# Ada-vector dot products with two load tiles of their own, and weight-keeping jobs with single buffers, in a two-layer trunk kernel

## The chip, the cores and the metric

The kernel runs on one core of a Trainium2 chip. The metric is the device time of one execution in microseconds (us). Three timed runs of the kernel before gave 2517.2, 2519.7 and 2522.97 us; their median, 2519.7 us, is the time before.

## The reference

The reference is a decoder trunk for one sequence of 1024 tokens with 1024 channels, in float32. Layer A is a diagonal state-space (S5) mixer with a gated linear unit (GLU) behind it; layer B is stick-breaking attention with 16 heads, whose keys and values come from the residual stream after layer A. Each layer ends with a squared-ReLU MLP of width 4096. Every sub-layer is normed and then shifted and scaled by vectors that come from one conditioning vector `c`:

```python
sh_a, sc_a, g_a, sh_m, sc_m, g_m = ada_chunks(c, ada_w[i], ada_b[i], 6)   # silu(c) @ ada_w[i] + ada_b[i]
h = modulate(rms_norm(x, mix_norm_g[i]), sh_a, sc_a)
mix = val * sigmoid(gate)            # layer A: val, gate = split(gelu(s5(h)) @ s5_w_glu)
x = x + g_a * mix
h = modulate(rms_norm(x, mlp_norm_g[i]), sh_m, sc_m)
x = x + g_m * (square(relu(h @ mlp_w1[i])) @ mlp_w2[i])
```

The products of `silu(c)` with the columns of the ada weights, 14 vectors of 1024 values in all, are matrix-vector products. So are the bias vectors that shift the keys, values and queries.

## The kernel before

The residual stream lies transposed in on-chip memory, as 8 channel tiles by 2 token halves (`xs[k][h]`, 128x512). All large products run on TensorE with every operand split into a rounded part and a rest (`uh` and `ul` for weights, hi and lo for activations), three matmuls for one (`mm3`). A weight unit is 128x1024: `load_unit` loads it on SyncE's queue (SP) into a `raw` tile (512 KB), ScalarE casts it to `uh` (L217), and VectorE subtracts to `ul` (L84). The raw tiles are a ring of three (`raw_tile`), the split ones a ring of three each (`un_tile`).

The stages follow each other: the S5 layer (its instructions in an order written out by hand, `S5_ORDER`, to about 212 us), the GLU (`glu`, 8 channel tiles by 2 halves, to about 417 us), the first MLP (`mlp(0, ...)`, to about 1145 us), the attention (to about 1793 us), its output projection and the second MLP. The first MLP begins with eight half units of up-products (one weight unit each, for one half), and then has 8 blocks `c`; each block is four up units and four down units, in the order in which they are written. Outside the S5 layer nothing but the attention's TensorE stream is pinned to the order written: a planner lays out the order of instructions on each engine by a simulated timeline when the program is built. On the chip each engine then runs its instructions in that fixed order.

Two kinds of side jobs are strewn between the units of the GLU and the first MLP:

- A dot product (`gemv`, L174) loads 128 columns of the transposed ada weights (or of the key, value and query weights) as a 128x1024 raw tile on SP and multiplies it by the broadcast row `silr` with a sum on VectorE (L177). There are 120: 96 on `adaT` and 24 on `wT`. An add of the bias (`fin`) closes each group of eight; `scale_cols` makes scales of some.
- A keeping job (`keep`, L224) prepares half a unit of the attention's weights on GpSimd (POOL): a load from POOL's queue into an `e` tile (L231), a scaling (L78, for keys, values and queries), a cast (L236), a subtraction (L84), and two stores to DRAM (`kh`, `kl`, L239), from which `fetch` takes them in the attention. There are 64. They use four `e` tiles, two for the first half of a unit and two for the second.

`queue` interleaves two jobs of the first kind with one of the second into the list `side`; `pump(n)` emits the next n of them. The GLU pumps nine after each channel tile from the second on, the MLP's `mid` three or four in turn after each down unit and after three of a block's up units. Everything left is emitted in `place(0)` in block 7, behind which the pools `b` and `e` are closed and the pool `late` is opened in their place.

A pool opened with `reuse_waits="tile"` (the helper `tile_pool`, L95) lets a tile wait only for the earlier tiles that lay in the same memory; the default lets it wait for the whole earlier pool that lay there.

Of the kernel before, what the change touches and what calls it, by code (L numbers as in the profile page):

```python
# [8 lines left out]
F32 = mybir.dt.float32  # L9
# [47 lines left out]
def kernel(ctx, tc, A, out):  # L57
# [4 lines left out]
    class Engine:  # L62
        def __init__(self, eng):
            self.eng = eng
# [15 lines left out]
    def add(o, a, b, eng=V):  # L80
        eng.tensor_tensor(o, a, b, op=ALU.add)  # L81
# [13 lines left out]
    def tile_pool(name, bufs=1, **k):  # L95
        return tc.tile_pool(name=name, bufs=bufs, reuse_waits="tile", **k)
# [7 lines left out]

    def open_x(i):
        es = ExitStack()
        pools["x"] = es.enter_context(tile_pool(f"xp{i}", bufs=16 if i else 1))
        pools["raw"] = es.enter_context(tile_pool(f"raw{i}", bufs=3))
        es.callback(pools.pop, "raw")
        turns.clear()  # L110
        return es

    def open_ax(i):
        es = ExitStack()
        pools["ax"] = es.enter_context(tile_pool(f"pax{i}", bufs=4 if "pv" in pools else 6, space=PSUM))
        return es

    cnt = [0]
# [1 line left out]
    def nm(s):  # L120
        cnt[0] += 1
        return f"{s}_{cnt[0]}"
# [9 lines left out]

    def open_pv():
        es = ExitStack()
        pools["pv"] = es.enter_context(tile_pool("ppv", bufs=2, space=PSUM))
        es.callback(pools.pop, "pv")
        return es

# [9 lines left out]
    def raw_tile():  # L148
        return pools["raw"].tile([P, 1024], F32, tag="raw", name=nm("raw"))
# [21 lines left out]
    silc = cp.tile([P, 8], F32, name="silc")  # L171
    kqs = single[:, 1:2]

    def gemv(src, row, bcol):  # L174
        raw = raw_tile()
        SP.dma_start(raw, src)
        V.tensor_tensor_reduce(raw, raw, row, 1.0, 0.0, op0=ALU.mult, op1=ALU.add, accum_out=bcol)  # L177

    def ada_chunk(c0, after=None):
        def one(i):  # L180
            gemv(A["adaT"][i - 16], silr, mod[:, i:i + 1])
# [6 lines left out]
        return [(lambda i=i: one(i)) for i in range(c0, c0 + 8)] + [fin]  # L188

    side = []  # L190

    def pump(n):
        for _ in range(min(n, len(side))):
            side.pop(0)()

    def queue(jobs, n, others):
        while jobs or others:
            side.extend(jobs[:n] + others[:1])
            del jobs[:n], others[:1]
# [24 lines left out]
    def keep(key, src, c, scale=None):  # L224
        if c == 0:
            kept[key] = [dp.tile([P, 1024], F32, name=nm(name)) for name in ("kh", "kl")]
        cs = slice(HN * c, HN * c + HN)
        while len(keeps) < 4:
            keeps.append(fs0.extra((F32, F32R)[len(keeps) % 2]))
        raw, hi = keeps[0:2] if c == 0 else keeps[2:4]  # L230
        G.dma_start(raw, src[:, cs])  # L231
        if scale is not None:
            nk = scale.shape[1] // 2
            r3 = raw.rearrange("p (k m) -> p k m", k=nk)
            mul(r3, r3, scale[:, nk * c:nk * c + nk].unsqueeze(2).broadcast_to([P, nk, HN // nk]), G)
# [25 lines left out]

    def s5(hook):
        es = ExitStack()
        sp = es.enter_context(tile_pool("sp", bufs=1))
        pp = es.enter_context(tile_pool("s5ps", bufs=2, space=PSUM))

        cst = sp.tile([P, C_N], F32, name="cst")
        SP.dma_start(cst, A["cst"])
# [609 lines left out]
    class Inner:  # L878
# [4 lines left out]

        def open(self, name):
            self.es[name] = ExitStack()
            self.pools[name] = self.es[name].enter_context(tile_pool("fp" + name))

        def close(self, *names):
            for name in names:
# [26 lines left out]
    def mlp(layer, xs, hs, norm, fs, mid=None, done=None, place=None):  # L916
# [135 lines left out]
        for h in range(2):  # L1052
            for f in range(4):
                u = load_unit(w1[f])
                plain(0, f, h, up(f, u, h))
                if h == 0 and f == 0:
                    norm.rstd(1)
                elif h == 0 and f == 1:
                    norm.spread(1)
                    norm.apply(1, 0, 8)  # L1060
# [422 lines left out]
        return oh, ou[-2:]  # L1483


    pools["un"] = ctx.enter_context(tile_pool("unp", bufs=3))
# [4 lines left out]
    rowp = ada_es.enter_context(tile_pool("rowp", bufs=1))  # L1491
    silr = rowp.tile([P, D], F32, name="silr")

    def gate(i):
        c = M_GA0 + i
        gemv(A["adaT"][c - 16], silr, mod[:, c:c + 1])
        add(mod[:, c:c + 1], mod[:, c:c + 1], adab[:, c:c + 1])

    first = []

# [19 lines left out]
    ordered[0] = False  # L1520
    hs = [[None, None] for _ in range(8)]
    fs = fs0 = Inner()
    fs.open("a")
    fs.open("e")
    norm = Norm(norm_tiles(fs), xs, hs, 2, M_SHM0)
    with tile_pool("gp", bufs=1) as gp:
        queue(ada_chunk(M_SHM0) + ada_chunk(M_SCM0, lambda: scale_cols(2, M_SCM0)) + ada_chunk(M_GM0), 2,
              [(lambda i=i, c=c: keep(("o", i), A["wo"][i], c)) for i in range(8) for c in range(2)])

        def glu(i, ug, uv, h):  # L1530
            ps = ps_pv if h == 1 and i <= 5 else ps_mm
            pg, pv = ps(), ps()
            for k in range(8):
                mm3(pg, ug, k, ys[k][h], k == 0, k == 7)
            if (i, h) == (6, 1):
                norm.spread(0)
                norm.apply(0, 0, 8)
            for k in range(8):
                mm3(pv, uv, k, ys[k][h], k == 0, k == 7)
            g = gp.tile([P, HN], F32, tag="g", name=nm("g"), bufs=3)  # L1540
# [34 lines left out]
        ts1(kqs, kqs, 0.125, ALU.mult)  # L1575

    def bias_jobs(lo, hi):
        return [(lambda i=i: gemv(A["wT"][i], silr, bias[:, i:i + 1])) for i in range(lo, hi)]

    pump(99)  # L1580
    side.extend(ada_chunk(M_KSC, lambda: scale_cols(4, M_KSC)) + ada_chunk(M_SCA1, lambda: scale_cols(1, M_SCA1)))
    queue(ada_chunk(M_KSH) + ada_chunk(M_SHA1) + ada_chunk(M_GA1) + ada_chunk(M_SHM1)
          + ada_chunk(M_SCM1, lambda: scale_cols(3, M_SCM1)) + ada_chunk(M_GM1)
          + [lambda: shift_row(M_KSH)] + bias_jobs(0, 16)
          + [lambda: shift_row(M_SHA1)] + bias_jobs(16, 24) + [kq_gain], 2,
          [(lambda hp=hp, n=n, c=c: keep(("kv", hp, n), A["wkv"][hp, n], c, scl[:, 32 + 4 * n:36 + 4 * n]))
           for hp in range(8) for n in range(2) for c in range(2)]
          + [(lambda hp=hp, c=c: keep(("q", hp), A["wq"][hp], c, scl[:, 8:16])) for hp in range(8) for c in range(2)])

    brow = cp.tile([P, 2, 128], F32, name="brow")  # L1590

# [18 lines left out]

    def place(k):
        if k == 0:
            pump(999)
            fs.close("b", "e")
            late.append(late_es.enter_context(tile_pool("late", side="right")))
        return late_tile("sg")

# [169 lines left out]
```

## Time and profile before

| | |
|---|---|
| time, median of 3 runs | 2519.7 us (2517.2 to 2522.97) |
| profiled execution, its own time | 2516.43 us |
| span of the profiled execution | 2514.7 us |
| TensorE busy | 2350.6 us, 93% |
| VectorE busy | 1754.3 us, 70% |
| GpSimd busy | 909.5 us, 36% |
| mean granted TensorE clock | 0.974 of full speed |

The span goes from the first to the last instruction. A row of a group names the kernel line, the engine, the operation, the tiles (out<-in), the shape and the count, then the busy time, the mean ns of one, and the idle time of the engine just before them with what ended it. In a timeline row the first two numbers are the start and the length in us, and what stands in brackets is the idle time before it and its releaser. PEclk is the granted clock as a share of 2.4 GHz.

### The profile page before, as it was taken

Reading aid. Unit: us, or ns where it says so; the run is one execution under the profiler, and the core shown is the slowest. Engines: PE = TensorE matmul, PEld = TensorE weight load, DVE = VectorE, ACT = ScalarE, POOL = GpSimd, SP = SyncE. Lnnn points to the kernel's source line nnn. Section 1 sums busy time; section 2 is a strip of 40 time slices with the busy share of each in tenths; the row PEclk is TensorE's granted clock in tenths of the full one; section 3 lists DMA queues with packets and bytes.
Section 4 is the critical chain, followed back from the end, with each engine's and each line's share of the span. In section 5 each row is a group of like instructions: output and inputs, shape, how many; then the busy total and the mean of one; then the engine's idle time right before and its main releaser. Section 6 shows DMA issues by size and latency. Waiting matters only on the chain.

```text
span 2514.7 us, 33271 instructions
## 1 busy us (share of the span) xinstructions
PE 2350.6 (93%) x12552; PEld 1979.3 (79%) x12552; DVE 1754.3 (70%) x2570; ACT 941.8 (37%) x1710; POOL 909.5 (36%) x965
## 2 busy tenths in 40 slices
PE   3888999989999999999899999998999999999998
PEld 2677788867778888888888888887778888888886
DVE  7997557766776545345687877788583667876787
ACT  5653124211111222133566666676351232223221
POOL 4664460378775000014333323343110322342334
PEclk8899999999999999998999999999999999999999
DMA  4225863667766333123211111126721011111112
GB/s 150 86 79 188 283 221 105 216 241 251 252 239 217 101 117 126 45 89 102 81 58 39 64 68 68 59 100 213 250 78 57 34 51 59 60 42 51 56 54 76
DMA packets 105344, 297.08 MB, mean 118 GB/s; under 512 B 13280, under 2 KB 25568, under 8 KB 105184
## 3 DMA queue, kind: packets, MB, share of 16 engines
q1 hardware_dynamic: 87264, 240.42, 27.9%
q0 software_dynamic: 15360, 50.34, 5.5%
q10 hardware_dynamic: 2560, 4.20, 0.7%
q8 instruction: 99, 1.62, 0.3%
q14 instruction: 61, 0.50, 0.1%
HBM read 241.23 MB, written 49.48 MB: 116 GB/s over the span
## 4 chain that ended last, share of the span: by engine, by line
PE 61%; DVE 17%; DMA 11%; issue 5%; ACT 2%; POOL 1%; SPq 0%; DVEq 0%; POOLq 0%; ACTq 0%
DMA raw<-in_adaT_dram 8%; PE pm L70 8%; PE pm L251 8%; PE pm L252 8%; PE pm L253 8%; PE pa L1001 3%; PE pa L999 3%; PE pa L1000 3%; PE pt L70 3%; DVE sn L1282 3%; DVE raw L177 2%; PE pa L253 2%; PE pa L251 2%; PE pa L252 2%; PE po L70 2%
## 5 line engine op out<-in xcount | busy, mean ns | idle before, releaser
L251 PE MATMUL pm<-h,uh 128*128 128x512 f32 x1192 | 465.6, 393 | 19.3 <-ACT rb L927 15.8
L253 PE MATMUL pm<-h,ul 128*128 128x512 f32 x1192 | 465.5, 391 | 4.7 <-DVE ul L84 4.7
L252 PE MATMUL pm<-h,uh 128*128 128x512 f32 x1192 | 466.3, 391 | 1.6 <-DVE h L93 1.6
L217 ACT CAST uh<-raw 128x1024 fp32r<-128x1024 f32 x130 | 136.7, 1051 | 486.9 <-PE pa L252 154.5
L84 DVE TENSOR_TENSOR ul<-raw,uh 128x1024 fp32r<-128x1024 f32 (+1 forms) x158 | 202.7, 1283 | 126.5 <-ACT uh L217 103.8
L251 PEld LDWEIGHTS pm<-h,uh 128*128 128x128 f32 x1192 | 225.0, 189 | 71.5 <-ACT rb L927 19.3
L177 DVE CUSTOM_DVE_ANT_0 raw<-raw,silr 128x1024 f32<-128x1024 f32 x119 | 162.5, 1369 | 155.4 <-DMA raw<-in_adaT_dram 140.6
L253 PEld LDWEIGHTS pm<-h,ul 128*128 128x128 f32 x1192 | 225.1, 189 | 52.5 <-DVE ul L84 5.6
L252 PEld LDWEIGHTS pm<-h,uh 128*128 128x128 f32 x1192 | 225.3, 189 | 48.6 <-DVE h L93 2.2
L70 PE MATMUL pm<-uh,h 128*128 128x256 f32 x1024 | 238.5, 301 | 3.8 <-DVE rs L1138 3.0
L1282 DVE TENSOR_TENSOR_SCAN sn<-sn 128x768 f32<-128x768 f32 (+7 forms) x128 | 180.6, 1417 | 46.5 <-ACT sn L1277 45.2
L81 POOL TENSOR_TENSOR f<-f,f 128x512 f32<-128x512 f32 x30 | 44.0, 1468 | 397.3 <-ACT f L831 397.2
L70 PEld LDWEIGHTS pm<-uh,h 128*128 128x128 f32 x1024 | 181.7, 199 | 5.0 <-DVE rs L1138 3.4
L81 POOL TENSOR_TENSOR raw<-raw 128x256 f32<-128x256 f32 x28 | 26.0, 929 | 411.4 <-DVE ul L84 411.4
L251 PE MATMUL pa<-f,uh 128*128 128x512 f32 x396 | 154.4, 390 | 1.7 <-DVE xall L93 1.0
L252 PE MATMUL pa<-f,uh 128*128 128x512 f32 x396 | 154.1, 389 | 0.0
L253 PE MATMUL pa<-f,ul 128*128 128x512 f32 x396 | 153.7, 389 | 0.0
L70 PE MATMUL pm<-ul,h 128*128 128x256 f32 x512 | 148.7, 290 | 0.9 <-DMA ul<-kl 0.9
L78 POOL TENSOR_TENSOR sg<-sg,sn 128x512 f32<-128x512 f32 x64 | 93.0, 1453 | 122.5 <-DVE sn L1282 56.3
L70 PE MATMUL pm<-h,uh 128*128 128x512 f32 x402 | 133.7, 414 | 0.0
L93 DVE SCALAR_TENSOR_TENSOR x<-pa,mod,x 128x512 f32<-128x512 f32 x143 | 103.3, 743 | 43.5 <-PE pa L253 29.6
L1277 ACT ACTIVATE sn<-z,rrr 128x512 f32<-128x512 f32 (+1 forms) x192 | 111.6, 581 | 46.9 <-PE z L70 45.4
(380 smaller groups left out, 5497.7 us busy)
## 6 DMA issues: line engine op xcount, KB each, us to landing
raw<-in_w_dram SPq DMA_DIRECT2D x140, 512.0 KB, 3.3
raw<-in_adaT_dram SPq DMA_DIRECT2D x96, 512.0 KB, 3.7
uh<-kh SPq DMA_DIRECT2D x40, 512.0 KB, 4.2
ul<-kl SPq DMA_DIRECT2D x40, 512.0 KB, 4.0
kh<-e POOLq DMA_DIRECT2D x64, 256.0 KB, 2.7
kl<-e POOLq DMA_DIRECT2D x64, 256.0 KB, 3.6
raw<-in_wT_dram SPq DMA_DIRECT2D x24, 512.0 KB, 4.3
raw<-in_wglu_dram SPq DMA_DIRECT2D x20, 512.0 KB, 4.7
```

The lines of the kernel that those rows point to most:

```text
L70: return lambda *a, **k: tc.keep_in_program_order(f(*a, **k))
L78: eng.tensor_tensor(o, a, b, op=ALU.mult)
L84: eng.tensor_tensor(o, a, b, op=ALU.subtract)
L93: V.scalar_tensor_tensor(o, a, s, b, op0=op0, op1=op1)
L177: V.tensor_tensor_reduce(raw, raw, row, 1.0, 0.0, op0=ALU.mult, op1=ALU.add, accum_out=bcol)
L217: ACT.copy(uh, raw)
L251: T.matmul(ps, uh[:, sl], hi, start=first, stop=False)
L252: T.matmul(ps, uh[:, sl], lo, start=False, stop=False)
L253: T.matmul(ps, ul[:, sl], hi, start=False, stop=last)
L999: T.matmul(p, uh[:, sl], hi, start=(i == 0), stop=False)
L1277: ACT.activation(g[:, HN * hb + c0:HN * hb + HN], p[:, c0:], AF.Sigmoid, scale=pj.rr[:, 2, t, a:a + 1])
L1282: V.tensor_tensor_scan(g[:, s0:], g[:, s0:], g[:, s0:], 1.0, op0=ALU.mult, op1=ALU.bypass)
```

## The change

Dot products become objects of a class `Gemv` with a `load` of their own. They load into a tile `gv` with two buffers in a new pool `g`, no longer into the raw ring, which in the first part has two tiles in place of three. Two lists, `gems` and `keep_jobs`, take the place of `side`. `pump(ng, nk)` emits ng dot products (and the adds between them), emits the loads of the next two, and emits nk keeping jobs. In the GLU it is called after each half: three dot products in the first channel tile and two in the others, with one keeping job up to the third channel tile and two from the fourth on. In the MLP each of the eight first half units is followed by two dot products, and each `mid` emits two dot products and one keeping job. The gates 1 to 7 of the GLU and the key/value scale (`M_KSC`) move into the list of the GLU. The keeping jobs use two `e` tiles in place of four. Most pools go back from `reuse_waits="tile"` to the default; those of the attention and `late` keep it.

```diff
-        pools["x"] = es.enter_context(tile_pool(f"xp{i}", bufs=16 if i else 1))
-        pools["raw"] = es.enter_context(tile_pool(f"raw{i}", bufs=3))
+        pools["x"] = es.enter_context(tc.tile_pool(name=f"xp{i}", bufs=16 if i else 1))
+        pools["raw"] = es.enter_context(tc.tile_pool(name=f"raw{i}", bufs=3 if i else 2))
...
-    def gemv(src, row, bcol):
-        raw = raw_tile()
-        SP.dma_start(raw, src)
-        V.tensor_tensor_reduce(raw, raw, row, 1.0, 0.0, op0=ALU.mult, op1=ALU.add, accum_out=bcol)
+    def product_sum(raw, bcol):
+        V.tensor_tensor_reduce(raw, raw, silr, 1.0, 0.0, op0=ALU.mult, op1=ALU.add, accum_out=bcol)
+
+    class Gemv:
+        def __init__(self, src, bcol):
+            self.src, self.bcol, self.raw = src, bcol, None
+
+        def load(self):
+            if self.raw is None:
+                self.raw = fs0.pools["g"].tile([P, 1024], F32, tag="gv", name=nm("gv"), bufs=2)
+                SP.dma_start(self.raw, self.src)
+
+        def __call__(self):
+            self.load()
+            product_sum(self.raw, self.bcol)
...
-    def pump(n):
-        for _ in range(min(n, len(side))):
-            side.pop(0)()
...
+    def pump(ng, nk=0):
+        n = 0
+        while gems and (n < ng or not isinstance(gems[0], Gemv)):
+            job = gems.pop(0)
+            n += isinstance(job, Gemv)
+            job()
+        for job in [j for j in gems if isinstance(j, Gemv)][:2]:
+            job.load()
+        for _ in range(min(nk, len(keep_jobs))):
+            keep_jobs.pop(0)()
...
-        while len(keeps) < 4:
-            keeps.append(fs0.extra((F32, F32R)[len(keeps) % 2]))
-        raw, hi = keeps[0:2] if c == 0 else keeps[2:4]
+        if not keeps:
+            keeps.extend((fs0.extra(F32), fs0.extra(F32R)))
+        raw, hi = keeps
...
             for f in range(4):
                 u = load_unit(w1[f])
                 plain(0, f, h, up(f, u, h))
+                if mid is not None:
+                    mid(True)
...
-    fs.open("a")
-    fs.open("e")
+    for name in "age":
+        fs.open(name)
...
+        for i in range(1, 8):
+            gems.extend(gate(i))
+        gems.extend(ada_chunk(M_SHM0) + ada_chunk(M_SCM0, lambda: scale_cols(2, M_SCM0)) + ada_chunk(M_GM0)
+                    + ada_chunk(M_KSC, lambda: scale_cols(4, M_KSC)))
+        keep_jobs.extend((lambda i=i, c=c: keep(("o", i), A["wo"][i], c)) for i in range(8) for c in range(2))
...
             for h in range(2):
                 glu(i, ug, uv, h)
-                if i == 0:
-                    for c in range(1 + 3 * h, 4 + 4 * h):
-                        gate(c)
-            if i:
-                pump(9)
+                pump(2 + (i == 0), 1 + (i > 2))
...
-    cyc = [0]
-
-    def mid():
-        cyc[0] += 1
-        pump((3, 4)[cyc[0] % 2])
...
+    def mid(first=False):
+        pump(2, 0 if first else 1)
```

Left out are the default pools of the S5 layer (`sp`, `s5ps`), of PSUM (`pax`, `ppv`), of the split weights, rows and GLU (`unp`, `rowp`, `gp`) and of the MLP (`fpa`, `fpe`, `fpb`), which change as `xp` does, the lists of the same chunks for the MLP, and `fs.close("b", "e", "g")` in `place(0)`.

## Rows read from the trace of the kernel before

**Rows 1.** The page's first part: busy time, share of the span, instructions.
```profile
PE 2350.6 (93%) x12552; PEld 1979.3 (79%) x12552; DVE 1754.3 (70%) x2570; ACT 941.8 (37%) x1710; POOL 909.5 (36%) x965
```

**Rows 2.** Stretches: us; busy (count) of PE, PEld, DVE, ACT, POOL; PEclk; DMA; GB/s.
```profile
212.00:417.00 205.00, 196.83 (x915) 162.03 (x912) 118.37 (x161) 52.20 (x77) 89.18 (x98) 0.98 0.65 225
417.00:460.00 43.00, 42.05 (x193) 34.44 (x192) 36.23 (x61) 22.84 (x33) 0.00 (x0) 1.00 0.34 111
460.00:800.00 340.00, 320.41 (x1383) 260.20 (x1382) 235.66 (x271) 59.10 (x83) 249.22 (x286) 0.98 0.71 247
800.00:1100.00 300.00, 300.00 (x1342) 248.97 (x1341) 140.72 (x191) 66.12 (x91) 0.00 (x0) 1.00 0.27 93
```

**Rows 3.** Waits of the whole span: us, times, longest.
```profile
DVE raw L177 <- DMA raw<-in_adaT_dram: 140.6, 72, 12.5
...
PEld pm L251 <- ACT rb L927: 19.3, 8, 6.9
```

**Rows 4.** Timeline of VectorE and of SyncE's queue in the loop of jobs.
```profile
576.74 1.21 DVE L84 TENSOR_TENSOR ul<-raw,uh 128x1024 fp32r<-128x1024 f32 x1
...
582.50 1.23 DVE L177 CUSTOM_DVE_ANT_0 raw<-raw,silr 128x1024 f32<-128x1024 f32 x1 [1.06 <-DMA raw<-in_adaT_dram]
...
587.50 1.23 DVE L177 CUSTOM_DVE_ANT_0 raw<-raw,silr 128x1024 f32<-128x1024 f32 x1 [3.10 <-DMA raw<-in_adaT_dram]
...
589.31 1.22 DVE L84 TENSOR_TENSOR ul<-raw,uh 128x1024 fp32r<-128x1024 f32 x1
...
577.98 6.11 SPq L176 DMA_DIRECT2D raw<-in_adaT_dram  x2
```

**Rows 5.** Groups by shape: busy, mean ns, idle before.
```profile
L177 DVE CUSTOM_DVE_ANT_0 raw<-raw,silr 128x1024 f32<-128x1024 f32 x119 | 162.5, 1369 | 155.4 <-DMA raw<-in_adaT_dram 140.6 <-DMA raw<-in_wT_dram 11.1 <-ACT silr L1571 3.3
```

**Rows 6.** Landing of the inputs' loads, and the chain's first and last such load.
```profile
DMA to landing us min/median/max: 3.0/3.7/7.4
...
280.15 6.03 DMA raw<-in_adaT_dram
...
457.69 4.74 DMA raw<-in_adaT_dram
...
786.09 3.37 DMA raw<-in_adaT_dram
```

**Rows 7.** First and last starts: keeping loads, and the MLP's first down products.
```profile
L231 POOL DMA_DIRECT2D e<-in_wkv_dram x32: 541/582/584, 374.7 to 683.1; - x32
...
L93 DVE SCALAR_TENSOR_TENSOR xall<-pa,mod,xall x79: 735/746/751, 478.8 to 1119.2; 128x512 f32<-128x512 f32 x79
```

**Rows 8.** Timeline at the start: the first two products and their second use.
```profile
23.00 9.16 PE L521 MATMUL pt<-raw,silc 128*128 128x256 f32 x32 [23.00 <-DMA raw<-in_ada_dram]
...
44.78 0.41 DVE L70 TENSOR_REDUCE su<-arow 128x16 f32<-128x256 f32 x1
```

**Rows 9.** ScalarE's cast at the S5 layer's end, and the stretch around it.
```profile
232.15 1.04 ACT L217 CAST uh<-raw 128x1024 fp32r<-128x1024 f32 x1 [11.75 <-DMA raw<-in_wglu_dram]
...
230.00:235.00 5.00, 1.52 (x11) 1.06 (x10) 2.62 (x4) 2.10 (x4) 0.00 (x0) 1.00 0.79 295
```

**Rows 10.** One keeping job on GpSimd, and the transfers' median landing.
```profile
590.47 1.03 POOL L78 TENSOR_TENSOR e<-e,scl 128x512 f32<-128x512 f32 x1 [1.98 <-DMA e<-in_wkv_dram]
...
594.51 0.54 POOL L239 DMA_DIRECT2D kl<-e  x1
...
kl<-e POOLq DMA_DIRECT2D x64, 256.0 KB, 3.6
e<-in_wkv_dram POOLq DMA_DIRECT2D x32, 256.0 KB, 3.4
```

**Rows 11.** The first writes of the late tiles.
```profile
L93 DVE SCALAR_TENSOR_TENSOR sg<-pv,mod,xall x4: 734/747/750, 1122.0 to 1143.6; 128x512 f32<-128x512 f32 x4
```

**Rows 12.** Timeline at the attention's end.
```profile
1792.95 0.39 PE L251 MATMUL pa<-h,uh 128*128 128x512 f32 x1
...
1793.55 0.43 DVE L81 TENSOR_TENSOR o<-po,ot 64x256 f32<-64x256 f32 x1 [0.51 <-ACT ot L1329]
```

More of the change, by code (lines that the diff above doesn't have):

```diff
@@ L114, in open_ax @@
         es = ExitStack()
-        pools["ax"] = es.enter_context(tile_pool(f"pax{i}", bufs=4 if "pv" in pools else 6, space=PSUM))
+        pools["ax"] = es.enter_context(tc.tile_pool(name=f"pax{i}", bufs=4 if "pv" in pools else 6, space=PSUM))
         return es
@@ L134, in open_pv @@
         es = ExitStack()
-        pools["pv"] = es.enter_context(tile_pool("ppv", bufs=2, space=PSUM))
+        pools["pv"] = es.enter_context(tc.tile_pool(name="ppv", bufs=2, space=PSUM))
         es.callback(pools.pop, "pv")
@@ L172 @@
     kqs = single[:, 1:2]
-    def gemv(src, row, bcol):
-        raw = raw_tile()
-        SP.dma_start(raw, src)
-        V.tensor_tensor_reduce(raw, raw, row, 1.0, 0.0, op0=ALU.mult, op1=ALU.add, accum_out=bcol)
+    def product_sum(raw, bcol):
[10 more added lines that the diff above has]
+            product_sum(self.raw, self.bcol)
     def ada_chunk(c0, after=None):
-        def one(i):
-            gemv(A["adaT"][i - 16], silr, mod[:, i:i + 1])
         def fin():
@@ L186, in fin @@
                 after()
-        return [(lambda i=i: one(i)) for i in range(c0, c0 + 8)] + [fin]
-    side = []
-    def pump(n):
-        for _ in range(min(n, len(side))):
-            side.pop(0)()
[L196 to L199, printed above, removed]
+        return [Gemv(A["adaT"][i - 16], mod[:, i:i + 1]) for i in range(c0, c0 + 8)] + [fin]
+    gems, keep_jobs = [], []
+    def pump(ng, nk=0):
[8 more added lines that the diff above has]
+            keep_jobs.pop(0)()
     def scale_cols(n, sc0):
@@ L263, in s5 @@
         es = ExitStack()
-        sp = es.enter_context(tile_pool("sp", bufs=1))
-        pp = es.enter_context(tile_pool("s5ps", bufs=2, space=PSUM))
+        sp = es.enter_context(tc.tile_pool(name="sp", bufs=1))
+        pp = es.enter_context(tc.tile_pool(name="s5ps", bufs=2, space=PSUM))
         cst = sp.tile([P, C_N], F32, name="cst")
@@ L885, in open @@
             self.es[name] = ExitStack()
-            self.pools[name] = self.es[name].enter_context(tile_pool("fp" + name))
+            self.pools[name] = self.es[name].enter_context(tc.tile_pool(name="fp" + name, bufs=1))
         def close(self, *names):
@@ L1483, in attention @@
         return oh, ou[-2:]
-    pools["un"] = ctx.enter_context(tile_pool("unp", bufs=3))
+    pools["un"] = ctx.enter_context(tc.tile_pool(name="unp", bufs=3))
     x_es = open_x(0)
@@ L1490 @@
     ada_es = ExitStack()
-    rowp = ada_es.enter_context(tile_pool("rowp", bufs=1))
+    rowp = ada_es.enter_context(tc.tile_pool(name="rowp", bufs=1))
     silr = rowp.tile([P, D], F32, name="silr")
@@ L1495, in gate @@
         c = M_GA0 + i
-        gemv(A["adaT"][c - 16], silr, mod[:, c:c + 1])
-        add(mod[:, c:c + 1], mod[:, c:c + 1], adab[:, c:c + 1])
+        if i == 0:
+            raw = raw_tile()
+            SP.dma_start(raw, A["adaT"][c - 16])
+            product_sum(raw, mod[:, c:c + 1])
+            add(mod[:, c:c + 1], mod[:, c:c + 1], adab[:, c:c + 1])
+            return []
+        return [Gemv(A["adaT"][c - 16], mod[:, c:c + 1]),
+                lambda: add(mod[:, c:c + 1], mod[:, c:c + 1], adab[:, c:c + 1])]
     first = []
@@ L1522 @@
     fs = fs0 = Inner()
-    fs.open("a")
-    fs.open("e")
+    for name in "age":
+        fs.open(name)
     norm = Norm(norm_tiles(fs), xs, hs, 2, M_SHM0)
-    with tile_pool("gp", bufs=1) as gp:
-        queue(ada_chunk(M_SHM0) + ada_chunk(M_SCM0, lambda: scale_cols(2, M_SCM0)) + ada_chunk(M_GM0), 2,
-              [(lambda i=i, c=c: keep(("o", i), A["wo"][i], c)) for i in range(8) for c in range(2)])
+    with tc.tile_pool(name="gp", bufs=1) as gp:
+        for i in range(1, 8):
[3 more added lines that the diff above has]
+        keep_jobs.extend((lambda i=i, c=c: keep(("o", i), A["wo"][i], c)) for i in range(8) for c in range(2))
         def glu(i, ug, uv, h):
@@ L1577, in bias_jobs @@
     def bias_jobs(lo, hi):
[L1578 to L1588, printed above, removed]
+        return [Gemv(A["wT"][i], bias[:, i:i + 1]) for i in range(lo, hi)]
+    pump(0, 99)
+    keep_jobs.extend((lambda hp=hp, n=n, c=c: keep(("kv", hp, n), A["wkv"][hp, n], c, scl[:, 32 + 4 * n:36 + 4 * n]))
+                     for hp in range(8) for n in range(2) for c in range(2))
+    keep_jobs.extend((lambda hp=hp, c=c: keep(("q", hp), A["wq"][hp], c, scl[:, 8:16]))
+                     for hp in range(8) for c in range(2))
     brow = cp.tile([P, 2, 128], F32, name="brow")
@@ L1612, in place @@
         if k == 0:
-            pump(999)
-            fs.close("b", "e")
+            pump(999, 999)
+            fs.close("b", "e", "g")
             late.append(late_es.enter_context(tile_pool("late", side="right")))
@@ L1631, in done0 @@
                 norm1.apply(0, 2 * (k - 1), 2 * (k - 1) + 2)
-    cyc = [0]
-    def mid():
-        cyc[0] += 1
-        pump((3, 4)[cyc[0] % 2])
+    gems.extend(ada_chunk(M_SCA1, lambda: scale_cols(1, M_SCA1)))
+    for c0 in (M_KSH, M_SHA1, M_GA1, M_SHM1):
+        gems.extend(ada_chunk(c0))
+    gems.extend(ada_chunk(M_SCM1, lambda: scale_cols(3, M_SCM1)) + ada_chunk(M_GM1)
+                + [lambda: shift_row(M_KSH)] + bias_jobs(0, 16)
+                + [lambda: shift_row(M_SHA1)] + bias_jobs(16, 24) + [kq_gain])
+    def mid(first=False):
+        pump(2, 0 if first else 1)
     mlp(0, xs, hs, norm, fs, mid=mid, done=done0, place=place)
```

## The prediction

> **What bounds the kernel now.** I read the page's engine times first: TensorE is busy for 93% of the span [rows 1]. So the change can only give back what TensorE loses while the jobs run, and I cut the span into stretches to see how much that is [rows 2]. From 800 to 1100 us TensorE never pauses and 1342 matmuls take 300 us, 0.2235 us each; a unit of 48 matmuls then takes 10.7 us. Against that, the GLU's stretch (212 to 417 us) loses 205 - 196.8 = 8.2 us in pauses and, at a granted clock of 0.98, some 3.9 us more; 417 to 460 loses 1.0; 460 to 800 loses 19.6 in pauses and 6.4 by its clock of 0.98. The sum is **39 us**, the most that better-placed jobs can return.
>
> The waits say who loses them. VectorE waited 72 times, 140.6 us, for the inputs of dot products, and TensorE's longest waits in the MLP are behind the relu on ScalarE, whose tiles VectorE frees late [rows 3]. The timeline shows the loop [rows 4]: the subtraction to `ul` at 576.74 frees a raw tile, SP loads an input at 577.98, the product runs at 582.50, its tile takes the next input, which is multiplied at 587.50, and the next `ul` comes at 589.31. Two loads stand one behind the other in each unit, since the other raw tiles hold weights that wait for TensorE. That makes 12.6 us a unit where TensorE needs 10.7.
>
> **The change part by part.** *Dot products and their work.* Their number stays 120, at 1.37 us of VectorE each [rows 5]. Removed is the ring that they share with the weights: a weight load no longer stands behind a product, and two inputs are under way at once. A tile's cycle is its load's landing, the product and the turnaround. From one product to the next on a single tile 5.0 us passed [rows 4]; by the mean landing of the 44 such loads in the chain from 460 to 800 us, 173.8 us in all or 3.95 each [rows 6], plus 1.37 and about 0.2 it is 5.5 us for a pair, in place of 12.6.
>
> *Where they land in VectorE's order.* The code loads one step ahead, but the planner isn't held to that order, and it starts side work as soon as its tiles allow: keeping jobs for keys and values, written behind the first block's units, had loads at 374.7 us, 104 us before the first down product's sum at 478.8 [rows 7]. With a ring of their own, I expect 118 of the products (all but the one in the S5 layer and an odd one) to be drawn forward in the same way, from the S5 layer's end on, each pair close behind its loads. Then the distance that a load is ahead is the planner's landing time, not a step, and each pair costs what the chip's landing is longer than the planned one. That is not in the trace; its bounds are nothing (the planner counts 3.95 us) and 1.3 us a pair: 0.95 if it counts the fastest landing, 3.0 us [rows 6], and 0.35 more if one load in six takes the 6.03 us of the one at 280.15 [rows 6], since more are under way at once. I take 0.95 us, the fastest without such delays: 72 waits in 96 loads say that the plan is short [rows 3]. Over 59 pairs this is 56 us.
>
> From this comes off what TensorE doesn't feel: in the 43 us before 460 VectorE is already busy for 36.2 [rows 2] and written ahead of most products, so they stay out of some 7 pairs' time (-7 us); and the two pairs of PSUM tiles hold half a unit, 5.4 us, once (-5). That leaves **+44 us** of loss in place of the 39. If products stayed a whole step behind their loads, it would be nothing.
>
> *Raw ring of two.* Each weight unit needs its raw tile once in 10.7 us, for a load, a cast and a subtraction: nothing in the loop. At the start the second pair of ada loads has to wait for the first product, which begins at 23.00, and the second result is used at 44.78 [rows 8]; the 9 us of the products [rows 8] and a load's 4 us end by 40: nothing, hidden by VectorE's own preparation, and at most 4 us if that cover were gone. At the S5 layer's end a cast waited 11.75 us for a weight load that stood behind seven inputs on SP, and TensorE worked 1.5 of 5 us there [rows 9]; the weights may now go first. This is inside the 39 us.
>
> *Keeping jobs with single buffers.* A job's instructions from the scaling to the last store's issue take 594.51 + 0.54 - 590.47 = 4.6 us; its load lands in 3.4 us and its store in 3.6 [rows 10]. With one pair of tiles these follow each other: 11.6 us a job, more than a unit. In the MLP GpSimd does nothing else before block 7, so 48 jobs take 557 us from about 460 to 1017, and `late` first writes at 1122.0 [rows 11]: 105 us of cover. In the GLU the norm's sums of squares stand between the jobs on GpSimd, and ScalarE's next square waits for them; 16 half steps by 0.9 us is 14 us that GpSimd may fall behind, 0 if sums slip between. I take the middle, **+7 us**. The Trainium skill's page "Trainium Kernel Development and Optimization" (Best Practices) says to double-buffer so that transfers overlap with work; the chain of 11.6 us agrees with it, but nearly all of it lies off the path.
>
> *Pool waits.* A tile of a later pool now waits for a whole earlier pool. At the attention's end the output projection's first sum began at 1792.95 while the last PSUM reads ran from 1793.55 to 1793.98 [rows 12]: about **+1.5 us** (0 if another PSUM tile goes first, 5 if the loads behind it slip too). `gv` and `e` tiles wait for the S5 pool, which ends by the cast's time above: inside the other sums.
>
> **The sum.** 44 + 7 + 1.5 - 39 = +13.5 us. On the profiled execution's own 2516.4 us that is 2530; the runs' median stands 3.3 us above it, so I forecast **2533 us**, 0.5% slower. A measurement of this kernel can tell about 0.2%, 5 us, from no change.
>
> **The rivals.** *VectorE stops waiting (faster).* The planner's landing is long enough, or priority keeps products behind a step's sums, so that the input is there when its turn comes. For it speaks the shortened cycle, 5.5 us a pair instead of 12.6, and two products a step that would fit in a unit; against it the early keeping loads [rows 7] and the waits of before. TensorE keeps its 0.2235 us through the GLU and the MLP: 2519.7 - 39 + 1.5 = 2482; with a third of the loss left (59 x 0.3 = 18) 2500. I put it at 2482 to 2512. It decides over my forecast from a shortfall under about 0.7 us a pair, where 59 x 0.7 = 41 - 12 + 8.5 is no more than the 39.
>
> *The loss only moves (same).* The shortfall is that of the median to the fastest landing, 3.7 - 3.0 = 0.7 us [rows 6], and the sum comes to -1.2 us: 2518. The Trainium skill's page "DMA: Bandwidth & Descriptors" (Anatomy of one DMA) gives about 2.0 us and 436 KB per us, so an estimate of 3.2 us for 512 KB; a planner that counts so would be 0.75 us short of the 3.95 here, which is this rival.
>
> *The keeping jobs come late (slower).* If a job takes over (1122 - 460) / 48 = 13.8 us, the sums of block 7 wait for the pool of the `e` tiles, and each 0.1 us more costs 4.8 us: at 14.5 us some 34 us, 2554. For it speaks that transfers share engines with more inputs; against it the 105 us of cover.
>
> **How the numbers follow.** My forecast has 0.46, with a range of its own from a shortfall of 0.8 to 1.3 us a pair, 2525 to 2562; VectorE that stops waiting 0.38; a loss that only moves 0.12; late keeping jobs 0.04. Slower is 0.50, same 0.12, faster 0.38. The range over all goes from 2486, which leaves out the best tenth, to 2566, above the upper bound of the shortfall and short of a late end with it.
>
> **What would show it.** Right: products on `gv` for `adaT` in a dense row from about 230 us to about 550, waits for their inputs of a microsecond a pair and more, TensorE's matmuls per stretch below 44.7 in 10 us in the GLU, full speed from 600 on, keeping loads until about 1000 us. Wrong: products two in each unit up to 900 us, no waits for inputs, a full TensorE in the GLU; or pauses at 1122 us behind `late`; or a stall on SP at the S5 layer's end longer than before.

## The result and the profile after

The changed kernel takes 2542.14 us (2539.48 to 2543.36, median of 4 runs) beside 2518.45 us (2514.49 to 2522.97) of the kernel before on the same chip: a ratio of 1.0092, 95% interval 1.0073 to 1.0112. It is slower by 0.9%, some 24 us, where the forecast was slower by 0.5%. The span of the profiled execution is 2541.6 us, 26.9 more than before.

The first thing to read is where TensorE gained and lost. Here are the stretches of the kernel before, then of the changed one (us; busy and count of PE, PEld, DVE, ACT, POOL; PEclk; DMA; GB/s):

```profile
230.00:310.00 80.00, 73.37 (x308) 59.71 (x307) 42.37 (x59) 17.83 (x27) 35.02 (x39) 0.94 0.81 283
310.00:360.00 50.00, 48.46 (x214) 39.74 (x213) 27.39 (x31) 10.69 (x16) 32.20 (x37) 1.00 0.68 235
360.00:420.00 60.00, 60.00 (x278) 50.05 (x277) 37.09 (x53) 21.82 (x29) 16.72 (x19) 1.00 0.37 132
420.00:500.00 80.00, 79.05 (x352) 64.98 (x351) 64.76 (x100) 28.36 (x40) 17.60 (x17) 1.00 0.55 184
500.00:600.00 100.00, 91.71 (x394) 74.09 (x393) 65.43 (x76) 17.71 (x25) 77.37 (x90) 0.97 0.71 250
600.00:800.00 200.00, 188.70 (x815) 152.98 (x814) 139.19 (x151) 34.43 (x50) 154.25 (x181) 0.99 0.70 246
```

```profile
230.00:310.00 80.00, 80.00 (x358) 66.33 (x357) 45.79 (x69) 17.77 (x28) 25.45 (x28) 1.00 0.80 276
310.00:360.00 50.00, 42.99 (x175) 34.57 (x174) 31.00 (x46) 7.33 (x11) 19.07 (x19) 0.93 0.75 254
360.00:420.00 60.00, 50.42 (x201) 39.97 (x200) 45.67 (x69) 14.41 (x19) 21.77 (x22) 0.91 0.86 287
420.00:500.00 80.00, 53.02 (x187) 37.20 (x186) 76.04 (x121) 24.55 (x35) 29.71 (x35) 0.83 0.77 263
500.00:600.00 100.00, 100.00 (x442) 82.81 (x442) 64.72 (x83) 23.57 (x33) 45.31 (x50) 1.00 0.60 206
600.00:800.00 200.00, 200.00 (x885) 165.64 (x884) 92.29 (x95) 40.58 (x55) 102.71 (x112) 1.00 0.34 122
```

Counts are the fair measure, at the 0.2235 us a matmul of the prediction. The changed kernel does 50 more matmuls from 230 to 310 us and 118 more from 500 to 800: 37.5 us gained, the prediction's 39. From 310 to 500 it does 563 where the kernel before did 844: 281 fewer, **62.8 us lost**. The net, 25.3 us, is the difference in span but for 1.6 us. The losing part is less than a tenth of the run, and the last stretch of it holds more than half: 36.9 us between 420 and 500, where VectorE is busy for 76.0 of 80 us.

The products' own rows (first and last start of each kind of load, then the landing), which answer to [rows 3, 6]:

```profile
L175 DVE CUSTOM_DVE_ANT_0 gv<-gv,silr x119: 1208/1225/2314, 237.5 to 973.4; 128x1024 f32<-128x1024 f32 x119
L186 SPq DMA_DIRECT2D gv<-in_adaT_dram x95: 327/328/426, 233.9 to 541.3; - x95
L186 SPq DMA_DIRECT2D gv<-in_wT_dram x24: 327/328/328, 545.0 to 968.0; - x24
its engine sat idle before it (us, times) until:
  DMA gv<-in_adaT_dram: 85.8, 44
...
DMA to landing us min/median/max: 3.1/4.4/9.5
```

The inputs of `adaT` are loaded from 234 to 541 us, whatever step their code stands in. VectorE waits for them 44 times, 85.8 us, where it waited 72 times, 140.6 us, before. Where the waits lie matters. By 310 us VectorE has waited 42.2 us (11 times), and TensorE is busy for 80.00 of 80 us from 230 to 310 all the same. From 310 to 420 us it waits 33.5 us (22 times), and from 420 to 500 only 2.7 us (4 times).

The chain of work (shares of the stretch), from 310 to 420 us and then from 420 to 500, says what TensorE stands behind there:

```profile
by line: DMA gv<-in_adaT_dram 60.8%; DVE gv L175 18.2%; issue 7.8%; DMA raw<-in_wglu_dram 5.5%; DVE ul L84 3.2%; DVE g L78 1.7%; DVE xall L93 1.3%; DVE scl L93 1.1%; DVE mod L81 1.1%; DVE rw L93 1.1%; DVE mod L175 0.9%; DVEq L175 0.1%; DVEq
...
by line: DVE gv L175 27.1%; DMA gv<-in_adaT_dram 18.0%; DVE h L93 11.9%; DVE f L93 11.4%; DVE ul L84 7.1%; DVE ra L78 4.9%; issue 4.8%; PE pm L264 3.1%; PE pm L265 2.5%; DVE rw L93 2.4%; PE pm L263 1.7%; DVE f L84 1.6%; DVE rw L87 1.5%; DVE
```

Up to 420 us the inputs are most of the chain: VectorE stands before a product whose input has not landed, and TensorE's longest waits there are for the `ul` that comes behind it (10.0 us, 3 times). One such place:

```profile
343.65 1.23 DVE L175 CUSTOM_DVE_ANT_0 gv<-gv,silr 128x1024 f32<-128x1024 f32 x1 [3.17 <-DMA gv<-in_adaT_dram]
...
344.81 1.22 DVE L84 TENSOR_TENSOR ul<-raw,uh 128x1024 fp32r<-128x1024 f32 x1
...
346.08 0.80 PE L265 MATMUL pm<-h,ul 128*128 128x512 f32 x1 [4.83 <-DVE ul L84]
```

Late weights explain little of it: ScalarE's casts wait 4.8 us for them from 310 to 420. From 420 us on the products themselves are a larger share than their inputs. The timeline of VectorE and TensorE in the middle of that stretch:

```profile
443.06 0.50 PE L264 MATMUL pm<-h,uh 128*128 128x512 f32 x1 [1.39 <-DVE h L93]
...
446.71 0.74 DVE L93 SCALAR_TENSOR_TENSOR f<-xall,scl,f 128x512 f32<-128x512 f32 x1
447.37 0.74 DVE L93 SCALAR_TENSOR_TENSOR h<-f,mod,h 128x512 fp32r<-128x512 f32 x1
448.03 1.22 DVE L175 CUSTOM_DVE_ANT_0 gv<-gv,silr 128x1024 f32<-128x1024 f32 x1
448.17 0.50 PE L264 MATMUL pm<-h,uh 128*128 128x512 f32 x1 [1.05 <-DVE h L93]
...
449.25 0.74 DVE L93 SCALAR_TENSOR_TENSOR f<-xall,scl,f 128x512 f32<-128x512 f32 x1
449.92 0.74 DVE L93 SCALAR_TENSOR_TENSOR h<-f,mod,h 128x512 fp32r<-128x512 f32 x1
450.58 1.21 DVE L175 CUSTOM_DVE_ANT_0 gv<-gv,silr 128x1024 f32<-128x1024 f32 x1
450.71 0.49 PE L264 MATMUL pm<-h,uh 128*128 128x512 f32 x1 [0.89 <-DVE h L93]
```

This is the norm's stretch at the MLP's start. Each activation tile needs two VectorE instructions (`f`, then `h`, 1.5 us together), and six matmuls of TensorE need each tile (three for each of two units, 6 x 0.2235 = 1.3 us). A product of 1.2 us goes behind each pair, with no wait for its input in these rows, so a tile comes each 2.5 us and TensorE waits about 1 us for each.

### The profile page after: what moved, and what is told of

Same layout as the page of the kernel before. It is cut to its first block, busy times and chain, and to the rows that moved or that the text cites. A ratio compares the mean times of both kernels' runs of the same rounds, so it can differ in the third digit from the quotient of the medians.

```text
span 2541.6 us, 33286 instructions
## 1 busy us (share of the span) xinstructions
PE 2363.0 (93%) x12552; PEld 1986.5 (78%) x12552; DVE 1748.2 (69%) x2570; ACT 942.9 (37%) x1710; POOL 928.8 (37%) x965
## 4 chain that ended last, share of the span: by engine, by line
PE 69%; DVE 16%; DMA 6%; issue 3%; ACT 2%; POOL 1%; DVEq 0%; SPq 0%; ACTq 0%; POOLq 0%
PE pm L264 9%; PE pm L263 9%; PE pm L265 9%; PE pm L70 8%; DMA gv<-in_adaT_dram 5%; PE pa L263 4%; PE pa L265 4%; PE pa L264 4%; PE pa L1011 3%; PE pa L1013 3%; PE pa L1012 3%; PE pt L70 3%; DVE sn L1296 3%; PE po L70 2%; PE z L70 2%
## 5 line engine op out<-in xcount | busy, mean ns | idle before, releaser
L175 DVE CUSTOM_DVE_ANT_0 gv<-gv,silr 128x1024 f32<-128x1024 f32 x119 | 155.7, 1313 | 101.6 <-DMA gv<-in_adaT_dram 85.8
L263 PE MATMUL pa<-f,uh 128*128 128x512 f32 x404 | 157.3, 389 | 0.0
L264 PE MATMUL pa<-f,uh 128*128 128x512 f32 x404 | 157.2, 389 | 0.0
L93 DVE SCALAR_TENSOR_TENSOR x<-pa,mod,x 128x512 f32<-128x512 f32 x143 | 103.3, 742 | 45.0 <-PE pa L265 37.5
L84 DVE TENSOR_TENSOR wt<-pt,wt 128x512 fp32r<-128x512 f32 (+1 forms) x160 | 100.8, 630 | 36.3 <-ACT wt L1324 30.8
```

The lines of the kernel that those rows point to most:

```text
L84: eng.tensor_tensor(o, a, b, op=ALU.subtract)
L93: V.scalar_tensor_tensor(o, a, s, b, op0=op0, op1=op1)
L175: V.tensor_tensor_reduce(raw, raw, silr, 1.0, 0.0, op0=ALU.mult, op1=ALU.add, accum_out=bcol)
L263: T.matmul(ps, uh[:, sl], hi, start=first, stop=False)
L264: T.matmul(ps, uh[:, sl], lo, start=False, stop=False)
```

## The experiments

The theories as the expectations name them: the *placing* theory says that products drawn forward occupy VectorE and make it wait up to 500 us; its rivals put the loss in the keeping jobs' single buffers, in the pools, or in the inputs' loads alone. The kernel before, run beside these, had medians of 2521.8 to 2522.2 us, 3.3 to 3.8 us above the 2518.45 beside the changed kernel, so a difference in us between one of these runs and the changed kernel is good to about 4 us; the ratios, each to the kernel before that ran beside it, are the safer comparison.

**Two pairs of keeping tiles.**

```diff
-        if not keeps:
-            keeps.extend((fs0.extra(F32), fs0.extra(F32R)))
-        raw, hi = keeps
+        while len(keeps) < 4:
+            keeps.append(fs0.extra((F32, F32R)[len(keeps) % 2]))
+        raw, hi = keeps[0:2] if c == 0 else keeps[2:4]
```

> The changed kernel with the keeping jobs' two pairs of e tiles back. Placing theory (the dot products, drawn forward, occupy VectorE and make it wait until about 500 us): nothing of the 24 us is in the keeping jobs, so 2538 to 2545 us, with TensorE's matmuls between 300 and 500 us as few as in the changed kernel (607). Keeping theory (single buffers hold up GpSimd and with it the norm's sums): 2535 if my +7 us was right, 2520 if all of the loss is theirs.

Measured: 2565.86 us, ratio 1.017 (1.0154 to 1.0187): 24 us slower than the changed kernel by the medians, some 20 by the ratios. Both theories missed: undoing the single buffers makes it worse. TensorE's counts up to 420 us are like those of the changed kernel; the difference lies between 420 and 600:

```profile
420.00:500.00 80.00, 47.64 (x157) 34.18 (x155) 76.29 (x105) 20.84 (x30) 51.54 (x57) 0.74 0.77 260
500.00:600.00 100.00, 89.70 (x365) 71.49 (x366) 85.52 (x100) 19.84 (x27) 69.80 (x78) 0.93 0.85 281
```

GpSimd works 121 us there in place of 75, and VectorE's instructions take longer: from 420 to 500 us 105 of them fill 76.3 us, where 121 filled 76.0 in the changed kernel. The timeline shows why:

```profile
503.16 1.60 POOL L84 TENSOR_TENSOR e<-e,e 128x512 f32<-128x512 f32 x1
503.55 2.29 DVE L175 CUSTOM_DVE_ANT_0 gv<-gv,silr 128x1024 f32<-128x1024 f32 x1
...
507.18 1.21 DVE L175 CUSTOM_DVE_ANT_0 gv<-gv,silr 128x1024 f32<-128x1024 f32 x1
```

A product that starts beside GpSimd's subtraction takes 2.29 us, one with GpSimd idle 1.21. The Trainium skill's page "SBUF — State Buffer" (Who interferes with whom) says that a VectorE instruction with two inputs in on-chip memory contends with a GpSimd instruction that reads it, that the ports which they share are an exclusive lock, and that the order of issue decides who blocks. By that rule the product would end at 503.16 + 1.60 + 1.21 = 505.97; the row ends at 505.84, so it agrees within 0.13 us. This gave the *sharing* theory of two later runs: pairs let more keeping jobs run early, beside a VectorE that is already full.

**Tile waits in the pools.** All pools that the change moved to the default go back:

```diff
-        pools["x"] = es.enter_context(tc.tile_pool(name=f"xp{i}", bufs=16 if i else 1))
+        pools["x"] = es.enter_context(tile_pool(f"xp{i}", bufs=16 if i else 1))
```

> The changed kernel with reuse_waits="tile" back in every pool that had it. Placing theory: 2539 to 2543 us, at most the 1.5 us of the attention's end. Pool theory (new tiles wait for the whole S5 layer's or GLU's pools): the loads of the first dot products and the norm's tiles start earlier, and the time falls towards 2520.

Measured: 2540.66 us, 1.0073 (1.0058 to 1.0087). TensorE's counts from 310 to 500 us are 183, 207 and 179, in sum 569 beside 563. The interval overlaps that of the changed kernel, and the pools are not the cause of the loss. The first load of a product is issued at 218.78 us here and at 233.92 in the changed kernel, where SP waits 14.7 us for the S5 layer's last `pt` before it; that wait costs nothing that shows.

**Every product in its step.** Loads and products get an order edge to an instruction of their step; an edge sets only the order on one engine.

```diff
+    def behind(e):
+        return tc.issue_after(step[e]) if e in step else ExitStack()
...
-                SP.dma_start(self.raw, self.src)
+                with behind("sp"):
+                    SP.dma_start(self.raw, self.src)
...
-            product_sum(self.raw, self.bcol)
+            with behind("v"):
+                product_sum(self.raw, self.bcol)
...
-        SP.dma_start(raw, src)
+        step["sp"] = SP.dma_start(raw, src).ins
...
-            mul(r, r, r)
+            step["v"] = V.tensor_tensor(r, r, r, op=ALU.mult).ins
```

`step["v"]` is set in the same way at the GLU's product and at each down product's sum.

> The changed kernel with every load of a dot product issued behind its step's weight load on SP, and every product behind its step's last result on VectorE, so that each really is one step ahead. Placing theory: TensorE stays full from 310 us on, products two in a unit until about 950 us; the 24 us and most of the 39 us that the kernel before lost come back: 2480 to 2505. Keeping or pool theory: the loss stays, 2530 to 2545. Inputs theory (loads themselves are too slow, whatever their place): 2515 to 2540, with waits for inputs as long as before.

Measured: 2493.52 us, 0.9884 (0.9867 to 0.99). The placing theory holds. VectorE's waits for inputs from 212 to 520 us fall from 81.6 us (38 times) to 16.8 (10 times), and TensorE keeps what it gained elsewhere:

```profile
310.00:360.00 50.00, 50.00 (x222) 41.43 (x221) 33.03 (x38) 11.66 (x16) 24.94 (x29) 1.00 0.64 216
360.00:420.00 60.00, 57.80 (x270) 47.72 (x269) 42.61 (x68) 22.71 (x32) 23.77 (x29) 1.00 0.52 175
420.00:500.00 80.00, 72.41 (x305) 57.76 (x304) 63.53 (x92) 23.26 (x33) 19.03 (x23) 0.96 0.66 226
```

**Only the MLP's list in its steps.** As above for products listed after the GLU; the first eight half units have none, and the GLU's 39 are free.

```diff
-                if mid is not None:
-                    mid(True)
...
-    pump(0, 99)
+    pump(99, 99)
...
+    late_gems[0] = True
```

> The changed kernel with only the MLP's list of products held in its steps, and none of them in the first eight half units; the GLU's list of 39 is placed freely. Placing theory: the GLU's products still come dense until about 360 us, then none until the first block; the loss between 360 and 500 us goes (some 30 us of the loss there), a few us stay before 360: 2490 to 2515. If the loss came from waits for inputs in the GLU alone: 2530 or more. Keeping or pool theory: 2535 to 2545.

Measured: 2493.93 us, 0.9885 (0.9869 to 0.9901). From 310 to 360 us, where the GLU's list still comes dense, TensorE does 182 matmuls, as in the changed kernel (175); from 420 to 500 it does 338. So the larger part of the loss was from the MLP's products in the GLU's end and the norm's stretch.

**One gv tile.**

```diff
-                self.raw = fs0.pools["g"].tile([P, 1024], F32, tag="gv", name=nm("gv"), bufs=2)
+                self.raw = fs0.pools["g"].tile([P, 1024], F32, tag="gv", name=nm("gv"), bufs=1)
...
-        for job in [j for j in gems if isinstance(j, Gemv)][:2]:
+        for job in [j for j in gems if isinstance(j, Gemv)][:1]:
```

> The changed kernel with one gv tile in place of two and one load ahead. Placing theory: a product each 5.5 us and more instead of two, so half as many products lie between 310 and 500 us and VectorE is not full there: fewer buffers make it faster, 2495 to 2520, with products until about 950 us. Inputs theory (VectorE's waits for the inputs themselves make the loss): one tile makes every product wait for its whole landing: 2545 or more.

Measured: 2576.44 us, 1.0215 (1.0196 to 1.0235). The time is in the range of the inputs theory. Half of the placing theory showed: from 310 to 500 us TensorE does 637 matmuls, 74 more than in the changed kernel. But from 500 to 1000, where that lost nothing, there are now 378, 782 and 828 in place of 442, 885 and 900: 239 fewer, 53 us. Each product waits for its whole landing (131.7 us, 58 times, from 212 to 620). Waits for inputs cost there too; my expectation left them out.

**The MLP's keeping jobs later.**

```diff
-        G.dma_start(raw, src[:, cs])
+        with tc.issue_after(step["g"]) if "g" in step else ExitStack():
+            G.dma_start(raw, src[:, cs])
...
+                if layer == 0 and (h, f) == (1, 3):
+                    step["g"] = G.tensor_copy(mark, r[:, 0:1]).ins
```

> The changed kernel with the 48 keeping jobs of the MLP held on GpSimd behind the eighth first half unit (a copy of one column marks it). Sharing theory (VectorE's instructions take longer while GpSimd works: h<-f 912 ns in the changed kernel between 420 and 500 us, 747 in the kernel before): VectorE gets some 6 us back there and h<-f is near 750 ns: 2530 to 2537. Placing theory alone (only the products' own time counts): 2540 to 2544. Held jobs late at the attention: 2550 or more.

Measured: 2543.49 us, 1.0084 (1.007 to 1.0099): nothing gained. GpSimd's time from 420 to 500 us falls from 29.7 to 19.6 us and `h<-f` from 912 to 830 ns, but VectorE stays full (75.8 of 80 us) and TensorE does 187 matmuls, as before the edit. The five jobs left in that stretch are the GLU's, on `wo`, which the edit does not hold; only two of the MLP's had been there. So the run shows no more than that the MLP's jobs don't matter.

**The ring alone, in the kernel before.**

```diff
-        raw = raw_tile()
+        raw = (fs0.pools["g"].tile([P, 1024], F32, tag="gv", name=nm("gv"), bufs=2) if "fs0" in own
+               else raw_tile())
```

> The kernel before with one part of the change alone: dot products load into two gv tiles, the raw ring has two. Placing theory: the ring alone lets the products be drawn forward through the GLU and the MLP's start, and the four e tiles leave GpSimd's jobs there too, as in the run with two pairs: 2540 to 2570. Rival (the ring is good, the new order of jobs or the single buffers do the harm): 2480 to 2505.

Measured: 2563.88 us, 1.0172 (1.0156 to 1.0189), with 155 matmuls from 420 to 500 us: the same time as the changed kernel with two pairs. The ring of its own is the part of the change that does the harm as the planner uses it, and the rest of the change, by the first run the single buffers, gives 22 us of it back.

**The kernel before, in step.** Its raw ring of three stays; products and their loads get the order edges of the run in step.

```diff
-        SP.dma_start(raw, src)
-        V.tensor_tensor_reduce(raw, raw, row, 1.0, 0.0, op0=ALU.mult, op1=ALU.add, accum_out=bcol)
+        with behind("sp"):
+            SP.dma_start(raw, src)
+        with behind("v"):
+            V.tensor_tensor_reduce(raw, raw, row, 1.0, 0.0, op0=ALU.mult, op1=ALU.add, accum_out=bcol)
```

> The kernel before with its products held in their steps (load behind the step's weight load, product behind the step's last result), still on the raw ring of three. If the ring's sharing is what cost the 39 us (my reading of the loop of 12.6 us a unit): 2505 to 2535. If the order alone did: 2480 to 2500, as with the ring of its own.

Measured: 2689.78 us, 1.0671 (1.0651 to 1.069), far outside both. A product that is held behind its step keeps a raw tile, and the weights of the next units wait for it: between 500 and 700 us

```profile
ACT uh L224 <- DMA raw<-in_w_dram: 112.8, 10, 19.7
```

(who waited for whom, us, times, longest). TensorE in turn waits for those casts. On the shared ring, order is no remedy. That it needs a ring of its own is not quite shown: this kernel writes a load directly before its product, so the run also lacks the step of lead that the changed kernel's loads have.

**Two pairs, the MLP's keeping jobs later.** The edits of the first and the sixth run together.

> The changed kernel with two pairs of e tiles, and the MLP's 48 keeping jobs held behind the eighth first half unit. Sharing theory (the pairs cost 24 us because their jobs run on GpSimd beside a VectorE that is full, whose instructions then take 1.4 to 1.7 us in place of 1.2): with the jobs behind that stretch most of the 24 us goes, 2540 to 2552. If the pairs cost it in the GLU or through the transfers: 2558 to 2568.

Measured: 2540.86 us, 1.0069 (1.0046 to 1.0093): the 24 us of the pairs are gone, as the sharing theory has it. The jobs' transfers left that stretch together with their arithmetic, so the runs show that the jobs' place is the cause; that it is the sharing with VectorE rests on the durations. The run shows one thing more: from 420 to 500 us GpSimd does nothing here, the products take 1222 ns on average and VectorE waits 4.7 us for their inputs, and yet TensorE does 218 matmuls where the kernel before did 352. As far as these rows show, what is left there is mostly the products' own time.

**In step, and the norm's stretch left free.** The run in step without `mid(True)`:

```diff
-                pump(2 + (i == 0), 1 + (i > 2))
+                pump(3 + (h == 0 and i < 3), 1 + (i > 2))
...
-                if mid is not None:
-                    mid(True)
...
-    pump(0, 99)
+    pump(99, 99)
```

> The changed kernel with products in their steps, three or four in each half of the GLU and none in the first eight half units. Placing theory: the GLU's products each have a load a step ahead, and the norm's stretch has VectorE for itself; what remains of the run in step lost between 420 and 500 us (305 matmuls, 11.8 us) falls to that of the held run (338, 4.5 us): 2482 to 2490. If three products in a half unit of the GLU are too many: 2491 to 2500.

Measured: 2487.46 us, 0.9859 (0.9835 to 0.9883): the fastest, with 341 matmuls from 420 to 500 us. From 310 to 420 us it does 466 where the run in step did 492, so by the counts the gain is some 10 matmuls, 2.2 us. Its interval overlaps that of the run in step; a gain beside that run is not shown. (The 39 products of the GLU's list stand in the halves of its first six channel tiles here; in the changed kernel 26 do, and 13 come in the first eight half units.)

**In step, with two pairs.** The edits of the first and the third run together.

> The run in step with two pairs of e tiles. Sharing theory: longer instructions on VectorE cost nothing where it has gaps, so as the run in step, 2490 to 2500. If pairs cost by themselves (transfers or GpSimd's order): 2505 to 2520.

Measured: 2490.07 us, 0.9864 (0.9842 to 0.9887). The products still take longer beside GpSimd (1506 ns on average from 212 to 560 us), but VectorE has gaps for it, and it costs nothing.

**Four gv tiles.**

```diff
-                self.raw = fs0.pools["g"].tile([P, 1024], F32, tag="gv", name=nm("gv"), bufs=2)
+                self.raw = fs0.pools["g"].tile([P, 1024], F32, tag="gv", name=nm("gv"), bufs=4)
...
-        for job in [j for j in gems if isinstance(j, Gemv)][:2]:
+        for job in [j for j in gems if isinstance(j, Gemv)][:4]:
```

> The changed kernel with four gv tiles and four loads ahead (the e tiles' pool shrinks to the two that are used). Occupation theory (in the GLU and the norm's stretch the products' own 1.3 us on VectorE make the loss): products come no later, 2535 to 2560. Inputs theory (the waits for inputs make it, as one gv tile suggests): the waits of 82 us between 212 and 520 us fall below 40, and the time to 2500 to 2525.

Measured: 2522.96 us, 1.0006 (0.9992 to 1.0021): no change from the kernel before, at the upper end of the range of the inputs theory. The waits from 212 to 520 us fall to 30.7 us (10 times), of which 18.7 is the first:

```profile
310.00:360.00 50.00, 50.00 (x223) 41.40 (x221) 47.30 (x69) 9.37 (x14) 16.51 (x15) 1.00 0.97 344
360.00:420.00 60.00, 49.30 (x206) 39.63 (x204) 58.19 (x92) 16.76 (x23) 19.67 (x18) 0.86 0.92 327
420.00:500.00 80.00, 60.64 (x227) 46.05 (x228) 66.90 (x102) 26.74 (x40) 27.49 (x34) 0.83 0.73 255
```

This sizes the two causes roughly. With 4.0 us of waits from 310 to 500 us in place of 36.2, TensorE does 656 matmuls there: 93 more than the changed kernel, 20.8 us, and still 188 fewer than the kernel before, 42 us. By this run about a third of the loss was waiting for inputs, and two thirds are products that stand in VectorE's order where TensorE needs it. The split is an estimate, since four tiles also move the products: 69 of them start from 310 to 500 us, where the changed kernel has 61, and the last `adaT` load is issued at 454.5 us in place of 541.3. The changed kernel's own stretches point the same way: 25.9 us were lost from 310 to 420 us, with 33.5 us of waits, and 36.9 us from 420 to 500, with 2.7.

## Why the prediction was right, and where its sum was off

The sign was right, and so was where the loss would come from: the products on `gv` were drawn forward into a dense row from 234 to 541 us, VectorE waited for inputs, TensorE lost in the GLU and ran full from 500 us on, and the ring alone, put into the kernel before, shows the loss by itself. What a product costs there was only partly right: the prediction priced the wait for its input, and the larger part of the loss was the product's own time on VectorE, which the prediction put at nothing. That the sum came as near as it did is in part luck. Term by term:

- *The 39 us that come back* came back: 37.5. The stall at the S5 layer's end [rows 9] is gone; TensorE is busy for 80.00 of 80 us from 230 to 310.
- *+44 for 59 pairs* was the mis-sized term; with the +7 it stood at 51 where 62.8 was lost, and its parts were off in opposite directions. The shortfall was longer than 0.95 us a pair: of the 85.8 us of waits 18.8 is the first, before a load that SP issued only behind the S5 layer's last `pt`, and the other 67 over 47 pairs on `adaT` make 1.4 us, above my upper bound of 1.3. But it counted less: about half of the 85.8 us lay before 310 us, where TensorE never paused, and taking nearly all of the waits away gave TensorE 20.8 us. What was left out is the product's own 1.2 us and more on VectorE; with four tiles and hardly a wait, 42 us were still lost. The step that failed is the cover: "in the 43 us before 460 VectorE is already busy ..., so they stay out of some 7 pairs' time (-7 us)". They did not stay out: from 417 to 460 us 13 products ran, where the kernel before had 4, and from 420 to 500 there were 24. This is the one stretch where TensorE lives from tile to tile on VectorE's `f` and `h`; the 16 `h` that VectorE makes for both halves took from 407.3 to 442.5 us before, and from 435.5 to 496.8 now. A busy engine was read as a place that work avoids; it was the place where each added instruction costs its whole length.
- *The 24 products on `wT`* were counted among those drawn forward; the first two loads were issued at 545 us, but the products ran from 852 to 973 us, since they need the shifted row `silr`, and cost nothing that shows.
- *+7 for single buffers* was wrong: with pairs the kernel is 20 to 24 us slower in this order and no different in step. The single pair slowed GpSimd, and in the crowded stretch that was a gain. The rest of that paragraph held: the last keeping load was issued at 1023 us and the last store at 1031 (1017 predicted) and `late` was first written at 1148.4, 26.4 after [rows 11], which is the delay from before 500 us and nothing of its own.
- *+1.5 for the pools* is within what the run with tile waits could tell (1.5 us between medians, 4.8 by the ratios, intervals overlapping); *the raw ring of two* cost nothing: up to 310 us TensorE is ahead of before.
- *The upper end of the range*, 2562 us, is more than the sum gives: at 1.3 us a pair it comes to 2554. The measured time is inside either.
- *The landing that the planner counts* stands in no trace, so the shortfall is known only by the waits that it left. The estimate of 3.2 us by the Trainium skill's page "DMA: Bandwidth & Descriptors" (Anatomy of one DMA) uses a fit that the page gives for transfers issued by GpSimd. The loads on SP's queue landed in 3.0 us at the fastest and 3.7 in the median before, and in 3.1 and 4.4 in the changed kernel.

The rival that VectorE stops waiting would have come out if the code's order had held. The run in step is that rival: 2493.5 us, within its 2482 to 2512. So the change is good by its idea and lost by its place.

## What to carry to other kernels

Give side work buffers of its own only together with an order: once nothing else holds it back, a planner puts it as early as its tiles allow, and "one step ahead" in the code says nothing about that. Before you cost added work at nothing, look for the stretch where TensorE lives hand to mouth on that engine; there, in this kernel, added instructions cost about their length even where nothing waited for an input. When a kernel gets slower with fewer waits, count matmuls per stretch on both sides before blaming the buffers that were cut: here cutting them had helped.

## What was not expected of the hardware

A two-input product on VectorE took 2.29 us beside GpSimd's subtraction in place of 1.21, and with two pairs some 24 us hung on where GpSimd's jobs ran, though TensorE needs none of their results for another 600 us. And the pauses cost TensorE clock as well: of the 38.2 us that the changed kernel lacks to full speed between 420 and 500 us (80 - 187 x 0.2235), 27.0 are pauses, and of the other 11.2 some 9 go with the granted clock of 0.83 (53.02 x 0.17); the rest is not accounted for. From 430 to 440 us, after a slice in which TensorE worked 5.03 of 10 us, the granted clock was 0.50, the lower level of 1.2 GHz:

```profile
420.00:430.00 10.00, 5.03 (x26) 3.83 (x24) 8.84 (x19) 2.26 (x3) 2.07 (x4) 0.89 0.82 288
430.00:440.00 10.00, 6.73 (x19) 5.21 (x20) 9.62 (x15) 2.36 (x4) 3.63 (x5) 0.50 0.77 266
```
